# A two-layer decoder step on one core: a new instruction order at the gates and the second head, and the first layer's mixing weights masked and summed in pieces on GpSimd

## The chip, the core and the metric

The kernel runs on one core of a Trainium2 chip. The core has five engines that run side by side, each with its own queue of instructions in order: TensorE (PE; PEld is its weight load), VectorE (DVE), ScalarE (ACT), GpSimd (POOL) and SyncE (SP), which here issues the DMAs. Engines wait for each other through semaphores. The metric is the device time of one execution in microseconds, as the median of several runs; the profile shows one profiled execution, whose span is the time from the first to the last instruction.

## The reference, cut to what matters

One inference step of a two-layer decoder for 256 prompt tokens and 8 x 8 sample tokens (320 columns in all), in float32. The first layer mixes tokens by a causal spatial-gating MLP in chunks of 128:

```python
h = gelu(x @ w_in);  u, v = split(h, 2)
v = layernorm(v) * ln_g + ln_b
ws = where(tril(ones(L, L)), w_s[:, :L, :L], 0)          # 8 groups, L = 128
mixed = einsum('gts,bnsgd->bntgd', ws, v) + b_s
y = (u * mixed) @ w_out
```

The second layer is an mLSTM with 8 heads. Its gates give, per token, the running sum `b` of log-sigmoids and the running maximum `m`; the heads use them as weights:

```python
D = b[:, None] - b[None, :] + i[None, :];  m = max(b + m_prev, max(D))
sc = (q @ k.T) * exp(D - m);  num = exp(b + m_prev - m) * (q @ C) + sc @ v
C_new = decay * C + (k * g).T @ v
```

`q` and `k` go through a causal width-4 convolution and silu, the head's output through a normalisation and a sigmoid gate `o`. Each layer is followed by a gated MLP with a width-3 convolution.

## The kernel before

**Tiling.** The activations stand transposed, features on partitions and the 320 tokens in columns. Every weight matrix is cut into blocks of 128 output rows by 8 x 128 inputs. Products are made to float32 accuracy from two rounded parts: ScalarE casts a loaded block `raw` to the high part `wh` (line 178), VectorE subtracts to get the low part `wl` (line 179), and TensorE adds three products per 128 inputs, high x high, high x low, low x high, so a block of 8 is 24 matmuls of 320 columns. `take` gives the next block in a fixed list and at that point traces the split of the block after it. In the second layer (`low_last`) a block does its 16 matmuls with `wh` first and its 8 with `wl` last. Three pairs of `wh` and `wl` are kept.

**Order.** The kernel is written with a scheduler that orders each engine's instructions by readiness and by the order in which they are traced. TensorE's instructions are pinned to the traced order. Three aids bend the rest: `behind(x, y)` puts x after y in their engine's queue; `with issue_after(y)` does this for everything traced in the block on y's engine; neither makes an engine wait for another. PSUM has eight banks: five tiles of tag `pa`, three of tag `pm`; the blocks of weights use `pm`.

**First layer.** The value half is made first (`group`, tile `pv_a`), then its statistics (`v_stats`: line 452 gives the reciprocal deviation `rstd` on GpSimd), `normalise` on ScalarE (line 458), and 16 blocks of the other half (tile `pm`), between which `mix` multiplies the normalised values with the masked mixing weights `ws` (128 x 8 groups x 128) and, for the samples, `wss`. `load_ws` loads these, masks them on GpSimd (lines 384 and 386), and sums `ws` over partitions into `rsum` (line 387), which `mix` uses with the layer norm's shift. In the profiled execution GpSimd does line 384, then 387, then 386.

**Gates and first head.** `gates` (lines 711 to 814) takes seven blocks in this order: q(0), v(0,0), k(0), v(0,1), o(0,0), o(0,1), and q(1) of the second head; the numbers are head and half. Among them VectorE works out the gate rows: two scans over tokens (line 766 the sum, line 771 the maximum, into `M`), `m` (772), `wi` (778, 779) and `g` (787, 788). ScalarE takes exponentials of them (780, 789, 790, 791) into `Xf` and `RS`. `Xf` is split into two rounded parts in `X` (783, 784), which one matmul broadcasts to all partitions (`pMb`); `RS` is turned by three transposes (`pt`) after q(1). The convolution of k(0) on VectorE is three times line 832 (the last is `S[0]["conv"]`), its product with the tanh is `q_` (836, 838), its split gives `kh` and `khl`; `low` in `gates` is that last subtraction. `last_low` is at any time the newest traced `wl`, `raised` is line 789.

**Later heads.** The loop at the end of `layer_b` does, for head h, the blocks of head h and the rest of head h-1 between them. For h = 1: k(1), v(1,0), `inter` and `numer` of head 0 (tile `num`), `state_prompt` (`pCp`), the first of four pairs of `state_sample` (`pcs`; VectorE's update of C, line 1067, frees the two banks, one of them of tag `pm`), v(1,1), o(1,0), the second pair, `scores(1)` (`psc`), o(1,1), the third pair, `finish(0)` (`phn`), the fourth pair, then the key transposes `k_nat` (`pk`, in a bank of tag `pm`) and `v_nat` (`pv`). `scores` ends with the split of the weighted scores into `Ph` and `Pl`; `o_epi` (line 1075) reads an output-gate block and so frees its bank; `v_epi` (855, 856) does so for a value block.

## Time and profile before

| what | value |
| --- | --- |
| median of 3 runs | 878.53 us (877.89 to 879.15) |
| profiled execution's own time | 878.1 us |
| its span | 876.4 us |
| granted TensorE clock | 0.999 |
| matmuls | 6388 |
| VectorE, ScalarE, GpSimd busy | 675.9, 505.8, 139.4 us |
| DMA | 155.74 MB, mean 178 GB/s |

A row of the timeline reads: start and duration in us, engine, line, operation, out<-in, shapes, how many instructions it merges, and in brackets the idle time of the engine before it and what ended it. The duration of an instruction overlaps that of its neighbours by some 0.07 to 0.16 us, so distances are taken from start to start. A row of the windows has the stretch, its length, and the busy time of PE, PEld, DVE, ACT and POOL with instruction counts, then TensorE's clock, the DMA share and GB/s.

### The profile page before, as it was taken

Reading aid. Unit: us, or ns where it says so; the run is one execution under the profiler, and the core shown is the slowest. Engines: PE = TensorE matmul, PEld = TensorE weight load, DVE = VectorE, ACT = ScalarE, POOL = GpSimd, SP = SyncE. Lnnn points to the kernel's source line nnn. Section 1 sums busy time; section 2 is a strip of 40 time slices with the busy share of each in tenths; the row PEclk is TensorE's granted clock in tenths of the full one; section 3 lists DMA queues with packets and bytes.
Section 4 is the critical chain, followed back from the end, with each engine's and each line's share of the span. In section 5 each row is a group of like instructions: output and inputs, shape, how many; then the busy total and the mean of one; then the engine's idle time right before and its main releaser. Section 6 shows DMA issues by size and latency. Waiting matters only on the chain.

```text
span 876.4 us, 16929 instructions
## 1 busy us (share of the span) xinstructions
PE 869.8 (99%) x6388; PEld 852.4 (97%) x6388; DVE 675.9 (77%) x1304; ACT 505.8 (58%) x917; POOL 139.4 (16%) x289
## 2 busy tenths in 40 slices
PE   9999999999999999999999999999999999999997
PEld 7899999999999999999999999999999999999997
DVE  6866986588878864559999997878998888786443
ACT  7557554455555544446868775656766555554442
POOL 3240000031000000015443222303003000000000
PEclk9999999999999999999999999999999999999999
DMA  8755645545545555554746876565664554455551
GB/s 270 228 193 166 184 146 180 175 148 170 163 155 167 164 163 156 167 177 149 239 147 217 255 226 221 188 211 172 196 218 148 170 168 150 163 163 166 157 151 60
DMA packets 54949, 155.74 MB, mean 178 GB/s; under 512 B 7460, under 2 KB 12716, under 8 KB 54868
## 3 DMA queue, kind: packets, MB, share of 16 engines
q1 hardware_dynamic: 54868, 154.67, 55.9%
q8 instruction: 50, 0.82, 0.4%
q14 instruction: 31, 0.25, 0.1%
HBM read 142.66 MB, written 11.99 MB: 176 GB/s over the span
## 4 chain that ended last, share of the span: by engine, by line
PE 97%; DMA 1%; DVE 1%; ACT 1%; issue 0%; POOL 0%; ACTq 0%
PE pm L81 84%; PE pv_a L81 6%; PE num L81 2%; PE pmix L81 1%; PE pcs L81 1%; PE pCp L81 1%; PE pv L84 1%; PE psc L81 1%; PE phn L84 1%; DMA out_Cp<-Cp 0%; DMA xT<-in_xv 0%; PE pk L84 0%; DVE y_p L665 0%; ACT hn L1039 0%; DVE wl L179 0%
## 5 line engine op out<-in xcount | busy, mean ns | idle before, releaser
L179 DVE TENSOR_TENSOR wl<-raw,wh 128x1024 fp32r<-128x1024 f32 (+4 forms) x254 | 302.7, 1194 | 109.0 <-ACT wh L178 106.2
L178 ACT CAST wh<-raw 128x1024 fp32r<-128x1024 f32 (+4 forms) x254 | 255.5, 1006 | 210.2 <-PE pm L81 146.9
L81 PE MATMUL pm<-xh,wh 128*128 128x320 f32 x1216 | 356.3, 301 | 0.0
L81 PE MATMUL pm<-xl,wh 128*128 128x320 f32 x1216 | 354.5, 299 | 0.0
L81 PE MATMUL pm<-xh,wl 128*128 128x320 f32 x1216 | 308.9, 299 | 0.0
L81 PEld LDWEIGHTS pm<-xh,wh 128*128 128x128 f32 x1216 | 229.9, 189 | 0.6 <-issue 0.5
L81 PEld LDWEIGHTS pm<-xl,wh 128*128 128x128 f32 x1216 | 229.9, 189 | 0.0
L81 PEld LDWEIGHTS pm<-xh,wl 128*128 128x128 f32 x1216 | 211.9, 189 | 0.1
L81 PE MATMUL pm<-yh_f,wh 128*128 128x320 f32 x352 | 105.2, 299 | 0.0
L81 PE MATMUL pm<-yl_f,wh 128*128 128x320 f32 x352 | 105.2, 299 | 0.0
L81 PE MATMUL pm<-yh_f,wl 128*128 128x320 f32 x352 | 105.2, 299 | 0.0
L81 PEld LDWEIGHTS pm<-yh_f,wh 128*128 128x128 f32 x352 | 66.5, 189 | 0.0
L81 PEld LDWEIGHTS pm<-yl_f,wh 128*128 128x128 f32 x352 | 66.5, 189 | 0.0
L81 PEld LDWEIGHTS pm<-yh_f,wl 128*128 128x128 f32 x352 | 66.5, 189 | 0.0
L569 DVE SCALAR_TENSOR_TENSOR fcv<-fpad,vecs,fcv 128x336 f32<-128x336 f32 x88 | 49.2, 565 | 1.4
L571 ACT ACTIVATE fgl<-fcv 128x256 f32<-128x256 f32 x44 | 18.2, 415 | 37.3 <-DVE fcv L569 37.3
L81 PE MATMUL pm<-yh_a,wh 128*128 128x320 f32 x128 | 38.4, 300 | 0.0
L81 PE MATMUL pm<-yl_a,wh 128*128 128x320 f32 x128 | 38.3, 299 | 0.0
L81 PE MATMUL pm<-yh_a,wl 128*128 128x320 f32 x128 | 38.3, 299 | 0.0
L323 DVE TENSOR_TENSOR xT<-pm,xT 128x320 f32<-128x320 f32 x39 | 19.1, 490 | 24.2 <-PE pm L81 24.2
L81 PE MATMUL pm<-yhb,wh 128*128 128x320 f32 x128 | 35.9, 304 | 0.0
L81 PE MATMUL pm<-ylb,wh 128*128 128x320 f32 x128 | 35.5, 300 | 0.0
(268 smaller groups left out, 1266.6 us busy)
## 6 DMA issues: line engine op xcount, KB each, us to landing
raw<-in_f_up SPq DMA_DIRECT2D x88, 512.0 KB, 3.5
raw<-in_b_win SPq DMA_DIRECT2D x48, 512.0 KB, 4.3
raw<-in_f_dn SPq DMA_DIRECT2D x32, 448.0 KB, 3.3
C<-in_C SPq DMA_DIRECT2D x32, 258.0 KB, 5.1
out_Cs<-C SPq DMA_DIRECT2D x32, 258.0 KB, 4.2
raw<-in_a_win SPq DMA_DIRECT2D x16, 512.0 KB, 3.8
raw<-in_a_wo SPq DMA_DIRECT2D x16, 512.0 KB, 4.0
raw<-in_f_dn SPq DMA_DIRECT2D x16, 512.0 KB, 3.5
```

What stands on the lines that cost most here:

```text
L81: self.pin(self.nc.tensor.matmul(out, lhsT, rhs, start=start, stop=stop, skip_group_check=skip))
L84: self.pin(self.nc.tensor.transpose(out, in_, ident))
L178: self.last_split = self.hold(nc.scalar.copy(wh[:, :kn, :], raw[:, :kn, :]))
L179: self.last_low = nc.vector.tensor_tensor(wl[:, :kn, :], raw[:, :kn, :], wh[:, :kn, :].bitcast(F32), op=SUB)
L323: self.nc.vector.tensor_tensor(x, ps[:, :T], x, op=ADD)
L569: nc.vector.scalar_tensor_tensor(cv, pd[:, i:i + NC], self.vec(w + i * KF), cv, op0=MULT, op1=ADD)
L571: nc.scalar.activation(gl[:, :TP], cv[:, :TP], AF.Gelu_apprx_tanh)
```

## The change

It has three parts. In the first layer the mask of `ws` is made in four instructions of two groups each, the sum over partitions too, and the sums are queued behind the last mask of `wss`. In the gates the copy of `Xf` to `X` (line 783) and the copy within `RS` (line 794) go from VectorE to GpSimd; the scan of line 771 is queued behind the newest `wl` at that point (that of o(0,1)), which was so for the last convolution step of k(0); line 784 is queued behind `low`; the edge to `again` goes. In the second head the scores come ahead of the second pair of `state_sample`, and `Pl` of the second head is queued behind the `o_epi` of o(1,1).

```diff
                 with tc.issue_after(self.rc_made.ins):
-                    nc.gpsimd.tensor_tensor(ws, ws, trit.unsqueeze(1).to_broadcast([P, NH, P]), op=MULT)
+                    pairs = [slice(g, g + 2) for g in range(0, NH, 2)]
+                    for g in pairs:
+                        nc.gpsimd.tensor_tensor(ws[:, g], ws[:, g], trit.unsqueeze(1).to_broadcast([P, 2, P]), op=MULT)
                     for r, c in quads:
-                        nc.gpsimd.tensor_tensor(wss[r, :, c], wss[r, :, c], bdt[r].unsqueeze(1).to_broadcast([64, NH, 64]), op=MULT)
-                    nc.gpsimd.partition_all_reduce(rsum.rearrange("p g t -> p (g t)"), ws.rearrange("p g t -> p (g t)"), P, ReduceOp.add)
+                        made = nc.gpsimd.tensor_tensor(wss[r, :, c], wss[r, :, c], bdt[r].unsqueeze(1).to_broadcast([64, NH, 64]), op=MULT)
+                    with tc.issue_after(made.ins):
+                        for g in pairs:
+                            nc.gpsimd.partition_all_reduce(rsum[:, g].rearrange("p g t -> p (g t)"), ws[:, g].rearrange("p g t -> p (g t)"), P, ReduceOp.add)
...
-                nc.vector.tensor_tensor_scan(M, rst[:8, 1, :], aM, -1e30, op0=ADD, op1=MAX)
+                scan = nc.vector.tensor_tensor_scan(M, rst[:8, 1, :], aM, -1e30, op0=ADD, op1=MAX)
...
-                nc.vector.tensor_copy(X[0:8], Xf)
-                nc.vector.tensor_tensor(X[32:40], Xf, X[0:8].bitcast(F32), op=SUB)
+                nc.gpsimd.tensor_copy(X[0:8], Xf)
+                Xl = nc.vector.tensor_tensor(X[32:40], Xf, X[0:8].bitcast(F32), op=SUB)
...
-                again = nc.vector.tensor_copy(RS[:64, T:384], RS[:64, TP:T])
+                again = nc.gpsimd.tensor_copy(RS[:64, T:384], RS[:64, TP:T])
...
-                self.behind(S[0]["conv"], self.last_low)
-                with tc.issue_after(S[0]["conv"].ins), tc.issue_after(raised.ins), tc.issue_after(again.ins):
+                self.behind(scan, self.last_low)
+                with tc.issue_after(S[0]["conv"].ins), tc.issue_after(raised.ins):
                     ps = self.block(KD, self.x_rhs)
                 for q_ in S[0]["q_"]:
                     self.behind(q_, self.last_low)
+                self.behind(Xl, low)
...
                 self.split(Ph[:, :384], Pl, Pf[:, :384])
+                s["Pl"] = self.parts[1]
...
             def o_epi(h, j, ps):
-                nc.vector.tensor_tensor(o, ps[:, :T], self.rb, op=MULT)
+                made = nc.vector.tensor_tensor(o, ps[:, :T], self.rb, op=MULT)
...
+                return made
...
                 if h == 1:
                     o_epi(h, 0, blk())
+                if h == 1:
+                    scores(h)
                 if h:
                     made = state_sample(h - 1, order[1])
...
-                scores(h)
+                if h != 1:
+                    scores(h)
...
                 if h and not last:
-                    o_epi(h, 1, blk())
+                    o_made = o_epi(h, 1, blk())
                 if h == 1:
+                    self.behind(S[1]["Pl"], o_made)
                     state_sample(0, order[2])
```

## The prediction

> **What bounds the kernel now.** I read the page first: its span and busy times.
>
> ```profile
> span 876.4 us, 16929 instructions
> PE 869.8 (99%) x6388; PEld 852.4 (97%) x6388; DVE 675.9 (77%) x1304; ACT 505.8 (58%) x917; POOL 139.4 (16%) x289
> ```
>
> TensorE is busy for 869.8 of 876.4 us. The change removes no matmul, so it can gain only what TensorE loses between matmuls in the stages touched, and lose only where it makes TensorE wait anew. A busy share hides small losses (matmuls overlap in the records), so I went through TensorE's timeline and compared the distance of neighbouring starts with the distance usual for that shape. The usual distances come from the chain of work in order of time (start, duration, what):
>
> ```profile
> 4.48 56.05 PE pv_a L81 x272
> 60.53 16.30 PE pm L81 x120
> ...
> 413.74 0.33 PE pt L84 x3
> ...
> 456.41 0.73 PE psc L81 x7
> ...
> 464.59 0.22 PE pcs L81 x2
> ```
>
> A 320-column matmul takes 16.30 / 120 = 0.136 us, one of the state update 0.22 / 2 = 0.11. In the first layer the value phase and the five blocks behind it join without a gap (4.48 + 56.05 = 60.53). So **the first layer has no TensorE loss that its part of the change could win back.** In the gates and in the second head the timeline shows three places:
>
> ```profile
> 408.92 0.30 PE L81 MATMUL pm<-xl,wh 128*128 128x320 f32 x1
> 409.13 1.35 PE L81 MATMUL pm<-xh,wl 128*128 128x320 f32 x8
> 410.32 0.30 PE L81 MATMUL pm<-xh,wh 128*128 128x320 f32 x1
> ...
> 432.22 0.27 PE L81 MATMUL pcs<-vh,kgz 128*128 128x258 f32 x1
> 432.90 0.38 PE L81 MATMUL pcs<-vh,kgz 128*128 128x258 f32 x1 [0.41 <-DVE C L1067]
> ...
> 437.95 0.47 PE L81 MATMUL pcs<-vb,kgz 128*128 128x258 f32 x2
> 438.53 0.55 PE L84 MATMUL pk<-ident,qs 128*128 128x128 f32 x3
> ...
> 464.34 0.47 PE L81 MATMUL pcs<-vb,kgz 128*128 128x258 f32 x2
> 464.65 0.49 PE L84 MATMUL pk<-ident,qs 128*128 128x128 f32 x3
> ```
>
> - **A**, in o(0,1), where the low parts of the weights begin: 408.92 to 409.13 is 0.21 where 0.14 is usual, and the first of the eight (1.35 us together, 0.27 + 8 x 0.135) takes about 0.10 more. Loss 0.17 us.
> - **B**, first head's state update: 432.22 to 432.90 is 0.68 instead of 0.11, and the second matmul is 0.38 instead of 0.27. Loss 0.57 + 0.10 = 0.67 us. It waits for VectorE's update of C, which frees the PSUM bank.
> - **C**, ahead of the second head's key transposes: 437.95 to 438.53 is 0.58; the third head does the same step in 0.31 (464.34 to 464.65); with 0.55 instead of 0.49 behind it, the loss is 0.33 us.
>
> A + B + C = **1.17 us, 0.13% of the time**: that is all that can be won. About 0.2%, 1.76 us, is what a measurement of this kernel can tell from no change.
>
> **The change part by part: the gates.** On VectorE and on ScalarE the stretch looks so:
>
> ```profile
> 406.37 0.54 DVE L832 SCALAR_TENSOR_TENSOR bcv<-bpad,vecs,bcv 128x344 f32<-128x344 f32 x1
> 406.84 0.48 DVE L772 TENSOR_TENSOR g<-g,Xf 8x320 f32<-8x320 f32 x1
> ...
> 407.87 1.20 DVE L179 TENSOR_TENSOR wl<-raw,wh 128x1024 fp32r<-128x1024 f32 x1
> 409.00 0.56 DVE L832 SCALAR_TENSOR_TENSOR bcv<-bpad,vecs,bcv 128x344 f32<-128x344 f32 x1
> 409.49 0.34 DVE L783 CAST X<-Xf 8x392 fp32r<-8x392 f32 x1
> ```
>
> ```profile
> 401.30 1.04 ACT L178 CAST wh<-raw 128x1024 fp32r<-128x1024 f32 x1
> ...
> 407.36 0.41 ACT L790 ACTIVATE RS<-g 8x256 f32<-8x256 f32 x1 [2.68 <-DVE g L772]
> ...
> 408.36 0.47 ACT L789 ACTIVATE RS<-g 8x320 f32<-8x320 f32 x1
> 408.85 1.05 ACT L178 CAST wh<-raw 128x1024 fp32r<-128x1024 f32 x1
> ```
>
> Loss A is the subtraction wl at 407.87: it ends at 409.07, and the low sweep of o(0,1) wants it at 408.92 + 0.14 = 409.06. Its own cast is old (401.30), so it could have run earlier. The change puts the scan (L771) behind this wl instead of the convolution's last step. The wl then runs two microseconds sooner and A goes: **-0.17 us**.
>
> The same edge delays the scan, m (L772), the rows behind it, and the exponentials on ScalarE, which wait for m (2.68 us idle at 407.36). Behind the last of them, `raised` (408.36), stands the cast wh at 408.85, which ends at 409.90 and is that of q(1); the edge that holds it there is kept. TensorE starts q(1) at 410.32, and 0.17 earlier without A: 410.15. So the cast has 0.25 us to spare. The delay of the scan is unknown; ends: if the wl takes the place of the convolution step at 406.37, 1.13 (its distance to the next start, 409.00 - 407.87) less 0.47 (406.84 - 406.37) = 0.66 us; if the third step, now free, slips in too, 1.13 + 0.49 = 1.62 us. The wait at q(1) is the delay less 0.25: **0.41 to 1.37 us**. I take the wl alone, the one row the new edge forces: 1.13 - 0.25 = **+0.88 us**.
>
> The copy of X (L783, 0.34 us) and a smaller one go to GpSimd, and Xl goes behind the key's low part. That frees VectorE after the exponentials, where the path runs through ScalarE's cast; I count nothing. Both ends of the copies are covered: their first reader is the transpose pt at 413.74, 3.9 us after X is copied now (409.83), and the broadcast of X comes later still; beyond that they would cost what they are late.
>
> **The second head.** VectorE's and ScalarE's rows:
>
> ```profile
> 432.37 0.47 DVE L1067 SCALAR_TENSOR_TENSOR C<-C,dec,pcs 128x258 f32<-128x258 f32 x1
> ...
> 437.39 0.56 DVE L334 TENSOR_TENSOR Pl<-Pf,Ph 128x384 fp32r<-128x384 f32 x1 [0.21 <-ACT Ph L334]
> ...
> 438.00 0.48 DVE L1075 TENSOR_TENSOR o_b<-pm,rb 128x320 f32<-128x320 f32 x1
> ```
>
> ```profile
> 433.09 0.21 ACT L856 COPY vTb<-pm 128x64 f32<-128x64 f32 x1
> ```
>
> With the scores ahead of the update, TensorE has 0.73 us of work (psc, seven matmuls) from 432.22, and the bank is free at 432.37 + 0.47 = 432.84, before the update comes at 432.95: B goes, -0.67. What is late next is the bank of o(1,1): TensorE now gets there at 432.95 + 0.22 = 433.17, and v(1,1) leaves its bank at 433.30. I add 0.10, between 0 and 0.20 (an eviction's end to the next start). Loss C is the wait for o_b (438.00 to 438.48), which frees the bank; it sat behind Pl. With Pl behind o_b, o_b can start at about 437.3 when its block is through, ends before 437.95, and C goes: -0.33. Pl is late by 0.45 us; its first reader, the next `numer`, stands behind two blocks of 24 x 0.136 = 3.26 us each. Together **-0.90 us**.
>
> **The first layer.** Here the question is only whether the new order makes something late.
>
> ```profile
> 34.69 3.36 POOL L384 TENSOR_TENSOR ws_a<-ws_a,trit 128x1024 f32<-128x1024 f32 x1 [3.54 <-DMA trit<-in_trit]
> 43.64 7.43 POOL L387 PARTITION_ALL_REDUCE rs_a<-ws_a  x1 [5.59 <-issue]
> 58.85 2.61 POOL L386 TENSOR_TENSOR wss_a<-wss_a,bdt 64x512 f32<-64x512 f32 x2 [7.78 <-issue]
> 67.55 0.91 POOL L452 TENSOR_TENSOR rstd_a<-ve_a,mhalf 128x3 f32<-128x3 f32 x1 [6.08 <-DVE ve_a L451]
> ```
>
> ```profile
> 34.59 4.54 DVE L179 TENSOR_TENSOR wl<-raw,wh 128x1024 fp32r<-128x1024 f32 x2 [0.23 <-ACT wh L178]
> ...
> 47.19 3.37 DVE L179 TENSOR_TENSOR wl<-raw,wh 128x1024 fp32r<-128x1024 f32 x1 [2.11 <-ACT wh L178]
> ...
> 72.02 1.22 DVE L179 TENSOR_TENSOR wl<-raw,wh 128x1024 fp32r<-128x1024 f32 x1 [2.45 <-ACT wh L178]
> ```
>
> A wl takes 1.2 us, but 3.37 beside the sum over partitions, and two take 4.54 beside the mask: GpSimd holds VectorE up, and pieces shorten the hold. TensorE loses nothing from it now, so that is worth 0. [...]
>
> What can be late is rstd (67.55). Two idle stretches without a releaser, 5.59 and 7.78 us, stand before and after the sum. Before, the second one ended 8.7 us ahead of rstd; in the new order it comes last. Masks 34.69 to about 42 (3.36 + 2.61 = 5.97 of work, and waits for one or two wl), then 5.6, the four sums R, then 7.8: GpSimd is ready at 55.4 + R. R lies between 7.43 (cost goes by size) and 4 x 7.43 = 29.7 (cost goes by call). I take the lower end with 2 us of waits for wl, R = 9.4, since the masks' cost goes by size; GpSimd is ready at 64.8, before 67.55: **0 us**.
>
> **Sum**: -0.17 + 0.88 - 0.90 = **-0.19 us**. Against the profiled execution's own 878.1 us (876.4 of span and 1.7 around it) that is 877.9; that execution lies 0.4 below the median of the runs, 878.5, so I forecast a median of **878.3 us**. With the ends of the unknown terms (0.41 to 1.37, 0 to 0.20) the sum goes from -0.76 to +0.40: 877.8 to 878.9.
>
> **The rivals.**
> - **R1, the gates cost nothing.** The scan's new place is paid from a step that moves behind it, and q(1)'s cast keeps its time. Against it: 0.25 us to spare and 0.66 at least. For it: the scan's neighbours (L832) are free to move. All three losses go: -1.07 to -1.17, 877.4 us.
> - **R2, the second head's waits come back elsewhere.** VectorE is nearly full there:
>
> ```profile
> 414.00:440.00 26.00, 25.48 (x205) 24.30 (x204) 25.04 (x64) 21.86 (x56) 11.70 (x25) 1.00 0.76 242
> ```
>
>   It is busy for 25.04 of 26.00 us, so another eviction may become late. Then the gates' 0.88 to 1.37 less 0.17 stays: +0.7 to +1.2, 879.2 to 879.7 us. Against it: the two waits have named releasers, and each is moved out of the way.
> - **R3, rstd becomes late (slower).** Its place is the first layer, 67 to 74 us:
>
> ```profile
> 68.68 1.52 ACT L458 ACTIVATE v_a<-v_a,ve_a,rstd_a 128x512 f32<-128x512 f32 x2 [2.06 <-DVE ve_a L453]
> ...
> 70.96 1.03 ACT L178 CAST wh<-raw 128x1024 fp32r<-128x1024 f32 x1
> ```
>
> ```profile
> 73.68 0.30 PE L81 MATMUL pm<-xh,wl 128*128 128x320 f32 x1
> ```
>
>   The normalisation waits for rstd, the cast at 70.96 stands behind it, the wl at 72.02 behind that, done at 73.24, and TensorE wants it at 73.68. So rstd has 0.4 us to spare; beyond 67.95 TensorE loses every microsecond. That is from R = 12.5, or 1.7 us of fixed cost for each sum after the first; at 3 us for each, R = 16.4 and the time is 4 us longer, 882 us. No row shows a second sum; against it speaks that the masks have hardly any fixed cost. If every sum brought its own 5.6 us, three more would make it 14 to 17 us, 892 to 895 us (1 in 100; the loads are pairs of instructions around a change of kind, and the sums follow each other). [...]
>
> **How the numbers follow.** Forecast 0.45, R1 0.26, R2 0.17, R3 0.12 (a quarter of it under 1.5 us). The range 877.0 to 880.0 takes in the forecast's ends, R1 and R2 with the 0.6 us by which runs of before differ from their median, and leaves out most of R3. Faster by over 0.2% (under 876.8) would need more than the three losses hold: 0.03, from R1. Slower by over 0.2% (over 880.3) is R3's larger part and a little of R2: 0.11. Within: 0.86.
>
> **What would show it.** Gates: the wl of o(0,1) ends before 408 and its low sweep starts without a gap; `raised` ends after 409.2, and TensorE waits for a cast ahead of q(1). If there is no such wait, R1 holds. Second head: seven score matmuls at the place of the 0.68 us step, and pk 0.3 us behind pcs. First layer: wl no longer over about 2.5 us; one idle stretch before the first sum, none between sums; rstd at 67.5. A rstd after 68 and a gap on TensorE near 73.7 would prove R3 and me wrong.

## The result and the profile after

The changed kernel takes **882.26 us** (median of 6 runs, 880.68 to 882.91) against 878.46 us for the kernel before (6 runs on the same chip, 877.89 to 879.15): a ratio of 1.0038, interval [1.0027, 1.005]. The change makes the kernel 3.8 us slower; 878.3 us had been forecast, and 880.0 us was the end of the range.

The page of the profiled execution (882.1 us by itself) begins with its span, and gives the busy time of each engine:

```profile
span 880.4 us, 16936 instructions
...
PE 870.2 (99%) x6388; PEld 852.4 (97%) x6388; DVE 673.8 (77%) x1302; ACT 506.6 (58%) x917; POOL 137.2 (16%) x297
```

The span is 4.0 us longer and TensorE is busy only 0.4 us longer, so the time went into new TensorE waits. The view of what the engines wait for lists them (waiting engine and line, releaser, total us, times, longest):

```profile
PE pm L81 <- ACT wh L178: 1.4, 1, 1.4
PE phn L84 <- ACT hn L1045: 1.3, 1, 1.3
PE pv_a L81 <- ACT v_a L417: 1.1, 1, 1.1
```

None of the three is in the profile before. The line numbers of the changed kernel are a little higher than those of before (the scan L775, `m` L776, the convolution L837, C's update L1073, `nb` L1038, `hn` L1045, `o_b` L1081). By the first layer's wait, everything in the second layer is also 1.34 us later than before: the convolution step at 405.15 is now at 406.49. Differences below are taken after that shift.

**At q(1).** TensorE's timeline around the wait, then VectorE's and ScalarE's:

```profile
410.39 1.25 PE L81 MATMUL pm<-xh,wl 128*128 128x320 f32 x8
413.02 0.40 PE L81 MATMUL pm<-xh,wh 128*128 128x320 f32 x1 [1.38 <-ACT wh L178]
```

```profile
406.49 0.56 DVE L837 SCALAR_TENSOR_TENSOR bcv<-bpad,vecs,bcv 128x344 f32<-128x344 f32 x1
406.98 1.21 DVE L179 TENSOR_TENSOR wl<-raw,wh 128x1024 fp32r<-128x1024 f32 x1
...
408.60 0.81 DVE L775 TENSOR_TENSOR_SCAN Xf<-rst,g 8x320 f32<-8x320 f32 x1
409.34 0.54 DVE L837 SCALAR_TENSOR_TENSOR bcv<-bpad,vecs,bcv 128x344 f32<-128x344 f32 x1
409.81 0.47 DVE L776 TENSOR_TENSOR g<-g,Xf 8x320 f32<-8x320 f32 x1
```

```profile
409.92 0.49 ACT L839 ACTIVATE bth<-bcv 128x344 f32<-128x344 f32 x1 [3.90 <-DVE bcv L837]
...
411.93 1.04 ACT L178 CAST wh<-raw 128x1024 fp32r<-128x1024 f32 x1
```

The eighth matmul of the first row starts at 411.34 and q(1) should start 0.14 behind it; it starts at 413.02, 1.54 us late, and its first matmul is 0.10 longer: **1.65 us**. VectorE shows why. The `wl` of 406.98 is ahead of the scan, and the convolution's third step (409.34), now free, has slipped in ahead of `m` as well. So `m` is 409.81 - 406.84 - 1.34 = 1.63 us later. On ScalarE the tanh `bth`, which stood behind the cast before, now runs ahead of the exponentials, and the cast `wh` starts 411.93 - 408.85 - 1.34 = 1.74 us later.

**In the second head.** TensorE's timeline, then VectorE's and ScalarE's:

```profile
435.37 0.56 PE L81 MATMUL psc<-qs 128*128 128x128 f32 x4
435.73 0.47 PE L81 MATMUL pcs<-vh,kgz 128*128 128x258 f32 x2
...
439.30 0.39 PE L81 MATMUL pcs<-vh,kgz 128*128 128x258 f32 x2
441.01 1.57 PE L84 MATMUL phn<-ident,hn 128*128 128x128 f32 x6 [1.32 <-ACT hn L1045]
442.34 0.47 PE L81 MATMUL pcs<-vb,kgz 128*128 128x258 f32 x2
442.64 0.49 PE L84 MATMUL pk<-ident,qs 128*128 128x128 f32 x3
```

```profile
436.57 0.48 DVE L1081 TENSOR_TENSOR o_b<-pm,rb 128x320 f32<-128x320 f32 x1
436.97 1.21 DVE L179 TENSOR_TENSOR wl<-raw,wh 128x1024 fp32r<-128x1024 f32 x1
438.10 0.55 DVE L905 SCALAR_TENSOR_TENSOR Pf<-psc,w 128x384 f32<-128x384 f32 x1
...
438.70 0.86 DVE L1073 SCALAR_TENSOR_TENSOR C<-C,dec,pcs 128x258 f32<-128x258 f32 x2
...
439.62 0.15 DVE L1038 SCALAR_TENSOR_TENSOR nb<-mv,sl 128x3 f32<-128x3 f32 x1
```

```profile
439.25 0.80 ACT L885 ACTIVATE w<-Mb,cols 128x256 f32<-128x256 f32 x2
...
440.39 1.48 ACT L1045 ACTIVATE hn<-num,nb,sl 128x256 f32<-128x256 f32 x3
```

In the profile before, the same steps on TensorE and VectorE were:

```profile
437.38 0.82 PE L84 MATMUL phn<-ident,hn 128*128 128x128 f32 x6
```

```profile
434.11 0.48 DVE L1075 TENSOR_TENSOR o_b<-pm,rb 128x320 f32<-128x320 f32 x1
434.51 0.87 DVE L1067 SCALAR_TENSOR_TENSOR C<-C,dec,pcs 128x258 f32<-128x258 f32 x2
435.29 0.15 DVE L1032 SCALAR_TENSOR_TENSOR nb<-mv,sl 128x3 f32<-128x3 f32 x1
```

B is gone: the two `pcs` matmuls now take 0.47 us together, behind the scores. C is gone: `pk` starts 0.30 behind the last `pcs`. In their place stands a larger wait. The second `pcs` of 439.30 starts at 439.41; the transposes `phn` should follow 0.11 later and start at 441.01, 1.49 us late; and the six take 1.57 instead of 0.82 us, because the three pieces of `hn` come one by one: **2.24 us**. Their input `hn` needs `nb`, and `nb` is queued behind the second pair's update of C. That update has moved with its matmuls behind the scores, and in VectorE's queue behind a `wl` and the scores' `Pf`. ScalarE adds to it: `nb` ends at 439.77, but `w` and a cast of `Ps` stand ahead of `hn`, which starts at 440.39.

**In the first layer**, GpSimd's sums and `rstd`:

```profile
46.79 7.42 POOL L391 PARTITION_ALL_REDUCE rs_a<-ws_a  x4 [6.05 <-issue]
68.51 0.90 POOL L456 TENSOR_TENSOR rstd_a<-ve_a,mhalf 128x3 f32<-128x3 f32 x1 [14.31 <-DVE ve_a L455]
```

GpSimd is done with the four sums at 54.21 and stands idle until `rstd`, whose releaser is VectorE's `ve_a`. The first layer's own wait comes from elsewhere, as ScalarE's and TensorE's timelines show:

```profile
22.25 1.04 ACT L178 CAST wh<-raw 128x1024 fp32r<-128x1024 f32 x1 [2.02 <-DMA raw<-in_a_wv]
```

```profile
32.72 0.38 PE L81 MATMUL pv_a<-wh,xh 128*128 128x512 f32 x1
34.19 0.48 PE L81 MATMUL pv_a<-wh,xh 128*128 128x512 f32 x1 [1.09 <-ACT v_a L417]
```

A block of weights came late: its cast stood 2.02 us for the DMA, and starts at 22.25 instead of 20.77, before the first instruction that the change touches. The squares behind it on ScalarE, `rc`, which is made from them, and `v_a`, which waits for `rc`, are late with it. TensorE lost about 1.36 us (34.19 - 32.72 - 0.21, and 0.10 of the next matmul).

| TensorE's loss (us), profiled executions | before | after |
| --- | --- | --- |
| A, low sweep of o(0,1) | 0.17 | 0 |
| q(1) | 0 | 1.65 |
| B, state update | 0.67 | 0 |
| `phn` | 0 | 2.24 |
| C, key transposes | 0.33 | 0 |
| first layer, late weights | 0 | 1.36 |
| sum | 1.17 | 5.25 |

The difference, 4.08 us, is that of the spans, 4.0.

### The profile page after: what moved, and what is told of

The parts are those of the page before. It is cut to its first block, busy times and chain, and to the rows that moved or that the text cites. A ratio compares the mean times of both kernels' runs of the same rounds, so it can differ in the third digit from the quotient of the medians.

```text
span 880.4 us, 16936 instructions
## 1 busy us (share of the span) xinstructions
PE 870.2 (99%) x6388; PEld 852.4 (97%) x6388; DVE 673.8 (77%) x1302; ACT 506.6 (58%) x917; POOL 137.2 (16%) x297
## 4 chain that ended last, share of the span: by engine, by line
PE 92%; DVE 3%; DMA 2%; ACT 1%; issue 1%; POOL 1%; SPq 0%; ACTq 0%; DVEq 0%
PE pm L81 82%; PE pv_a L81 3%; PE num L81 2%; DMA raw<-in_a_wv 2%; PE pmix L81 1%; DVE wl L179 1%; PE pcs L81 1%; PE pCp L81 1%; PE phn L84 1%; PE pv L84 1%; PE psc L81 1%; POOL nr L297 1%; ACT wh L178 0%; DVE bcv L837 0%; PE pk L84 0%
```

## The experiments

All times are medians, with those of the kernel before from the same chip beside them. The diffs are against the kernel before unless it is said otherwise, and `e2`, `e3` and so on stand for the full names.

### The three parts, each alone

`e1_first_layer_only`: the part in `load_ws`, nothing else.

```diff
-                    nc.gpsimd.tensor_tensor(ws, ws, trit.unsqueeze(1).to_broadcast([P, NH, P]), op=MULT)
+                    for g in pairs:
+                        nc.gpsimd.tensor_tensor(ws[:, g], ws[:, g], trit.unsqueeze(1).to_broadcast([P, 2, P]), op=MULT)
...
+                    with tc.issue_after(made.ins):
+                        for g in pairs:
+                            nc.gpsimd.partition_all_reduce(rsum[:, g].rearrange("p g t -> p (g t)"), ws[:, g].rearrange("p g t -> p (g t)"), P, ReduceOp.add)
```

> Only the first layer's part of the change. Theory: the 1.3 us that TensorE waits near 32.7 us in the profile of the changed kernel comes from a weight block that landed late (ScalarE's cast waited 2.02 us for it at 22.25), 10 us before GpSimd's first new instruction, so this part is worth nothing: median within 0.7 us of before, 877.8 to 879.2, rstd_a at about 67.5, no wait of TensorE near 73.7. Rival: the new GpSimd order makes the first layer slower: 879.7 to 880.2, with the wait near 32.7 in most executions.

Measured: 878.51 us against 878.47 (12 and 35 runs), ratio 1.0002 [0.9991, 1.0012]. Its profile has A, B and C as before and no wait near 32.7; `rstd` starts at 67.14. The theory held: the part is worth nothing either way.

`e2_gates_only`: the edits in `gates`, nothing else.

```diff
+                scan = nc.vector.tensor_tensor_scan(M, rst[:8, 1, :], aM, -1e30, op0=ADD, op1=MAX)
...
-                self.behind(S[0]["conv"], self.last_low)
-                with tc.issue_after(S[0]["conv"].ins), tc.issue_after(raised.ins), tc.issue_after(again.ins):
+                self.behind(scan, self.last_low)
+                with tc.issue_after(S[0]["conv"].ins), tc.issue_after(raised.ins):
```

> Only the gates' part. Theory: the scan behind wl, and with it the third convolution step and the tanh ahead of the exponentials, makes the cast of q(1)'s block 1.6 to 1.75 us later, TensorE waits about 1.6 us for it, loss A (0.17) goes, the second head's 1.0 us stays: 879.7 to 880.2. Rival: the second head's waits shrink by what TensorE came late: 878.5 to 879.0.

Measured: 880.25 us against 878.47, ratio 1.0018 [1.0008, 1.0028]. TensorE's timeline has the wait at q(1):

```profile
412.97 0.40 PE L81 MATMUL pm<-xh,wh 128*128 128x320 f32 x1 [1.37 <-ACT wh L178]
```

The theory's mechanism held. A is gone, but B has shrunk to 0.32 us, which it had not foreseen (the two `pcs` take 0.54 us to the next start, 0.22 without a wait).

`e3_head_only`: the edits in the second head, nothing else.

```diff
+                s["Pl"] = self.parts[1]
...
+                if h == 1:
+                    scores(h)
                 if h:
                     made = state_sample(h - 1, order[1])
...
-                scores(h)
+                if h != 1:
+                    scores(h)
...
-                    o_epi(h, 1, blk())
+                    o_made = o_epi(h, 1, blk())
                 if h == 1:
+                    self.behind(S[1]["Pl"], o_made)
```

> Only the second head's part. Theory: the update of C, and the row nb that is queued behind it, come behind a wl and the weighted scores on VectorE, so hn is late and TensorE waits about 2.2 us for it at the transposes phn, while the two old losses (0.67 and 0.33) go: 879.4 to 880.0. Rival: hn is late only because the gates made everything late; here alone the part gains 0.9: 877.3 to 877.9.

Measured: 880.51 us against 878.47, ratio 1.002 [1.0009, 1.003]. `hn` is late in this kernel too, with the gates and the first layer as before. The view of waits lists it, and no wait at q(1):

```profile
PE phn L84 <- ACT hn L1040: 1.4, 1, 1.4
```

The time is 0.5 us over the theory's range; four of the twelve runs belong to an upper group, of which more below.

The three medians add up: 0.04 + 1.78 + 2.04 = 3.86 us, and the whole change costs 3.80. Each part's interval reaches 0.9 us either way, so that the sums agree this closely is luck.

### The gates: the edge, and what stands behind it

`e4_gates_no_scan_edge`: as `e2`, but the convolution's last step and not the scan is queued behind the `wl`, as before.

```diff
-                self.behind(scan, self.last_low)
+                self.behind(S[0]["conv"], self.last_low)
```

> The gates' part without the edge on the scan: the last convolution step is behind wl as before, the two copies on GpSimd, Xl behind khl. Theory: the edge alone makes the wait at q(1), so without it the time is before's or up to 0.3 better, 877.9 to 878.7, loss A of 0.17 us still there. Rival: the copies on GpSimd make X or RS late and cost by themselves: above 879.2, with a wait of TensorE at pt or pMb.

Measured: 878.71 us against 878.47, ratio 1.0 [0.9991, 1.001]; its profile has no wait at q(1). The moves to GpSimd cost nothing that can be measured; the edge on the scan is the cost of the part. The moves also do something that the prediction put at nothing: B is only 0.19 us here. The next start is 433.82, so the two matmuls take 0.41 us instead of 0.22.

```profile
433.41 0.57 PE L81 MATMUL pcs<-vh,kgz 128*128 128x258 f32 x2
```

VectorE's update of C starts 0.33 us before the first of them (at 433.08); in the kernel before, it started 0.15 us after it. The two copies, 0.38 us from start to start (409.49 to 409.87), are off VectorE's queue. That this is what lets the update come earlier is argued from these distances and not tested alone.

`e6_gates_cast_free`: as `e2`, with the scan's edge, but q(1)'s cast is no longer held behind the exponentials.

```diff
-                with tc.issue_after(S[0]["conv"].ins), tc.issue_after(raised.ins):
+                with tc.issue_after(S[0]["conv"].ins):
                     ps = self.block(KD, self.x_rhs)
```

> The gates' part alone, as in e2_gates_only, but the cast of q(1)'s block is no longer queued behind the last of the exponentials on ScalarE. Theory (q(1) waits 1.53 us because its cast stands behind exponentials that the later scan has made late): the wait at 411.3 us goes although the scan stays late; A is gone; time 878.2 to 878.6 us, unless the exponentials' readers (pt, pMb behind q(1)) become late, which I put at 0 to 0.5 us. Rival (the scan's lateness itself costs, through the rows that TensorE needs next, or something else of this part does): TensorE waits over 1 us for RS or X at about 413 to 415 us, time 879.5 us or more.

Measured: 878.05 us against 878.78 (11 and 29 runs), ratio 0.9988 [0.9979, 0.9997]. ScalarE's timeline shows the cast ahead of the first exponential, which starts at 410.53:

```profile
409.60 1.03 ACT L178 CAST wh<-raw 128x1024 fp32r<-128x1024 f32 x1
```

TensorE waits for nothing between 404 and 416 us, although the scan is as late as in `e2`. So the later scan alone costs nothing: its readers `pt` and `pMb` have the time. What cost 1.65 us was a cast that needs none of the exponentials and stood behind them by an edge. A is gone in this profile, and so is all of B but 0.04 us, which had not been expected; most of B went already in `e4`. C stays.

### The second head: where nb stands

`e5_head_nb_early`: as `e3`, but the first head's `nb` and `hn` are queued behind the first pair's update of C.

```diff
                 if h == 1:
+                    with tc.issue_after(made.ins):
+                        normed(h - 1)
                     scores(h)
                 if h:
                     made = state_sample(h - 1, order[1])
-                    if not last:
+                    if not last and h > 1:
```

> The second head's part alone, as in e3_head_only, but the normalisation of the first head (nb, hn) is queued behind the FIRST pair's update of C, ahead of the scores, and no longer behind the second pair's. Theory (the part costs because nb and hn stand behind the update of C that the scores were put ahead of): the wait of phn for hn (2.36 us in e3_head_only) goes, the waits B (0.67 us) and C (0.33 us) of the kernel before go too, A (0.17 us) stays; span about 875.4 us, time 877.4 to 877.9 us (0.6 to 1.1 us under the kernel before). Rival (hn is late because VectorE and ScalarE are nearly full in this stretch whatever the order, so that another eviction takes the place): a new wait of TensorE of over 1 us between 432 and 442 us, time 879.0 us or more.

Measured: 881.05 us against 878.78, ratio 1.0028 [1.0017, 1.0039], slower than `e3`. The wait for `hn` is gone and another one of nearly the same size is there; C is not gone either (`pk` starts 0.87 us behind `pcs`). VectorE, ScalarE and TensorE in the profile (about 5 us later here, by a first-layer wait):

```profile
439.09 0.16 DVE L1033 SCALAR_TENSOR_TENSOR nb<-mv,sl 128x3 f32<-128x3 f32 x1 [0.84 <-POOL sl L1024]
```

```profile
439.29 0.56 ACT L1040 ACTIVATE hn<-num,nb,sl 128x256 f32<-128x256 f32 x1 [1.22 <-DVE nb L1033]
```

```profile
440.33 0.40 PE L81 MATMUL pm<-xh,wh 128*128 128x320 f32 x1 [1.66 <-ACT vTb L856]
```

`nb` was now too early: VectorE waited in it for GpSimd's `sl`, and on ScalarE the first piece of `hn` stood in front of the copies of v(1,1) (`vTb`, from 439.75), which free the bank that o(1,1) needs. The rival held for this order: an eviction became late. Whether any order does better is the next question.

`e9_head_nb_behind_o`: as `e3`, but `nb` directly behind the reading of o(1,0).

```diff
+                    o_first = o_epi(h, 0, blk())
                 if h == 1:
+                    with tc.issue_after(o_first.ins):
+                        normed(h - 1)
                     scores(h)
```

> The second head's part alone, as in e3_head_only, but nb of the first head is queued directly behind the reading of o(1,0) (o_b), instead of behind the second pair's update of C. In e3_head_only GpSimd has its input sl ready at 434.81 us and that o_b ends at 434.48, so VectorE stands for about 0.4 us ahead of a subtraction that nobody wants soon, and hn runs on ScalarE in the idle 1.13 us ahead of Ph, behind the copies of v(1,1). Theory (the 2.36 us wait of phn comes from nb's place in the queue alone; e5_head_nb_early failed only because it put nb ahead of wl and o_b, where it waited 0.84 us for sl and hn then held the copies of v(1,1)): the wait of phn goes, no other comes; B and C gone; span 875.4 to 875.9 us, time 877.3 to 877.9 us. Rival (the stretch has no room: any place of nb makes another eviction late): a new TensorE wait of over 1 us between 432 and 445 us, 879 us or more.

Measured: 879.07 us against 878.87 (12 and 29 runs), ratio 1.0004 [0.9996, 1.0013]: 1.8 us less than `e3` against the kernel before. The wait of `phn` and B are gone, and no wait of over 1 us has come in the second head; so the place of `nb`, and of `hn` behind it, is the cause. But the time is that of the kernel before and not 1 us less. VectorE and TensorE in its profile (about 3.5 us later by a first-layer wait):

```profile
438.49 0.16 DVE L1033 SCALAR_TENSOR_TENSOR nb<-mv,sl 128x3 f32<-128x3 f32 x1 [0.36 <-POOL sl L1024]
```

```profile
441.06 0.54 PE L81 MATMUL pcs<-vb,kgz 128*128 128x258 f32 x2
441.76 0.55 PE L84 MATMUL pk<-ident,qs 128*128 128x128 f32 x3 [0.16 <-DVE o_b L1076]
```

The 0.36 us in which VectorE stands for `sl` make all behind it late, `o_b` too, and `pk` starts 0.70 behind `pcs` again: C is back. Neither theory had that, though the time is the rival's.

### Loss C alone

`e7_pl_edge_only`: the kernel before, with `Pl` behind `o_b` alone.

```diff
+                    self.behind(S[1]["Pl"], o_made)
```

> The kernel before with one edge alone: Pl of the second head is queued behind the reading of o(1,1) (o_b). Theory: C (0.33 us ahead of the key transposes pk) goes and nothing else changes: span 876.0 to 876.1 us, ratio 0.9996. Rival (that wait comes back at a later place because VectorE is nearly full there): C goes and as much appears elsewhere behind it; span 876.3 us or more.

Measured: 879.20 us against 878.78, ratio 1.0009 [0.9999, 1.002]. C is gone at `pk`, and 0.44 us appear one block later (444.61 is 0.48 behind the last of the eight matmuls before it, instead of 0.14, and its first is 0.10 longer). TensorE and VectorE there:

```profile
443.18 1.25 PE L81 MATMUL pm<-xh,wl 128*128 128x320 f32 x8
444.61 0.40 PE L81 MATMUL pm<-xh,wh 128*128 128x320 f32 x1 [0.18 <-DVE C L1068]
```

```profile
443.12 1.04 DVE L1097 SCALAR_TENSOR_TENSOR ylb<-y_b,gnh,yhb 128x320 fp32r<-128x320 f32 x2 [0.95 <-ACT yhb L1096]
444.08 0.48 DVE L1068 SCALAR_TENSOR_TENSOR C<-C,dec,pcs 128x258 f32<-128x258 f32 x1
```

The fourth pair's second update of C frees the next block's bank. It stood behind `ylb`, and VectorE waited 0.95 us for ScalarE ahead of `ylb`. In the kernel before, loss C covered this.

A further 0.30 us is lost ahead of the block that follows `pv`: it starts 0.87 us after the first transpose of `pv` (440.03), in the kernel before 0.57. TensorE and VectorE:

```profile
440.90 0.40 PE L81 MATMUL pm<-xh,wh 128*128 128x320 f32 x1
```

```profile
439.52 0.54 DVE L334 TENSOR_TENSOR Pl<-Pf,Ph 128x384 fp32r<-128x384 f32 x1
439.99 0.86 DVE L1068 SCALAR_TENSOR_TENSOR C<-C,dec,pcs 128x258 f32<-128x258 f32 x2
```

`Pl` now stands ahead of the third pair's update of C, and the block starts right where that update ends (440.85). So the edge on `Pl` wins 0.33 and loses 0.30 + 0.44 us; the 0.41 us that this makes is close to the 0.42 of the medians, though the interval is wider than that. That the third pair's update is what this block waits for is read from the two times. The rival held.

### Versions put together

`e8_all_mended`: gates as in the change, but with the convolution's second step behind the `wl` in place of the scan; head as in `e5`.

```diff
+                self.behind(S[0]["conv2"], self.last_low)
...
+                    with tc.issue_after(made.ins):
+                        normed(h - 1)
                     scores(h)
```

> Both parts mended, the first layer as in the kernel before. Gates: the two copies on GpSimd and the split of X behind the key's low part stay, but it is the convolution's SECOND step, not the scan, that is queued behind the wl of o(0,1). Second head: scores early and Pl behind o_b as in the changed kernel, but the first head's normalisation is queued behind the first pair's update of C. Theory (each part loses only by what stands behind the instruction that was moved): A, B and C go and no wait takes their place; 1.17 us less than before, span 875.2 us, time 877.2 to 877.6 us, which is faster than both kernels. Rival (gates and second head are so full on VectorE that any order gives the losses back): 878.4 us or more.

Measured: 881.85 us against 878.78, ratio 1.0038 [1.0023, 1.0053]. At the second head it has the fault of `e5`. At q(1) TensorE waits again, and loses 1.29 us with the longer first matmul. A `wl` ahead of `m` is 1.13 us whatever edge puts it there, and the cast has 0.25 to spare; the tanh `bth`, which the convolution's earlier end lets in among the exponentials (409.08, 0.49 us), makes the cast later by some 0.4 more. Both mends were wrong, and by its time the rival held.

`e10_gates_and_head`: the gates of `e6` and the head of `e9`.

> The gates as in e6_gates_cast_free (the changed kernel's gates without the edge that holds q(1)'s cast behind the exponentials) and the second head as in e9_head_nb_behind_o; first layer as before. Theory: the two parts do not touch, A, B and C are all gone and no wait is left: span 875.2 to 875.5 us, time 877.0 to 877.5 us, faster than both kernels. Rival (the gates' part had already removed B by shifting the head's work, so that the head's part adds only its costs): as e6_gates_cast_free or slower, 877.9 us or more.

Measured: 878.15 us against 878.87, ratio 0.9995 [0.9986, 1.0004]; 0.72 us less, the same as `e6` alone, as the rival had it. A and B are gone and C nearly so, but 0.28 and 0.10 us stand where `e7` has its wait at `ylb`, and 0.30 us ahead of the block behind `pv`, as in `e7`.

`e12_last_pair_first`: as `e10`, and `ylb` behind the fourth pair's update of C (diff against `e10`).

```diff
                     finish(h - 1)
-                    state_sample(h - 1, 3)
+                    made = state_sample(h - 1, 3)
+                if h == 1:
+                    for y in S[0]["ylb"]:
+                        self.behind(y, made)
```

> As e10_gates_and_head, and in the second head the two subtractions ylb are queued behind the fourth pair's update of C. In e10_gates_and_head and e7_pl_edge_only TensorE waits about 0.45 us (0.28 and 0.10 at 441.93 in the former) for a bank that this pair's second update frees; the update stood behind ylb, which itself waited 0.88 us for ScalarE's yhb. Theory (C was won at pk and lost again there): that wait goes, span 875.4 to 875.6 us, time 0.9 to 1.2 us under the kernel before, that is 877.6 to 877.9 us if the kernel before is at 878.8. Rival (the next step is bound by something else, the casts on ScalarE or the bank of another tile): TensorE loses as much within the next 3 us and the time is that of e10_gates_and_head, 0.7 us under the kernel before.

Measured: 877.83 us against 878.81 (12 and 29 runs), ratio 0.9988 [0.9976, 1.0], 0.98 us less. VectorE does both of this pair's updates in one stretch from 439.65, ahead of `ylb` (440.99), and the wait that the other update had caused is gone: the theory held. Of C about 0.1 us is left at `pk`, and the 0.30 us ahead of the block behind `pv` (438.86) stay, since the third pair's update is still behind `Pl`. This version is faster than both kernels by its median, though the interval reaches to no change.

`e11_after_cast_free`: the changed kernel with the one edge of `e6` less. `e13_after_both_mended`: that, and `nb` as in `e9`.

> The changed kernel whole, with one edge less: q(1)'s cast is not held behind the exponentials. Theory: its 1.65 us wait at q(1) goes and everything else stays, the 2.2 us at phn too: 1.5 to 1.7 us less than the changed kernel's 882.3, that is 880.5 to 880.8 us. Rival (with the cast early, the exponentials and what reads them become late in the whole change): 881.5 us or more.

> The changed kernel whole with both queue places mended: q(1)'s cast not held behind the exponentials (as in e11_after_cast_free) and nb directly behind the o_b of o(1,0) (as in e9_head_nb_behind_o). The first layer in pieces stays. Theory (the two queue places are all that the change costs): as e10_gates_and_head, 0.6 to 0.8 us under the kernel before. Rival (the first layer's part costs something that shows only in the whole change): 0.8 us or more over that, slower than the kernel before.

Measured: `e11` 879.08 us against 878.87, ratio 1.0005 [0.9996, 1.0015]; `e13` 877.82 us against 878.81, ratio 0.9987 [0.9977, 0.9998]. With both places in the queues mended, the whole change, first layer included, is about 1 us faster than the kernel before. `e11` came out 1.4 us below its theory's lower end, on which the next runs bear.

### The rest: the granted clock

`e14_changed_again`: the changed kernel.

> The changed kernel, unchanged, again. Its six runs fell into two groups, 880.7 (two runs) and 882.1 to 882.9 (four), and its profiled run, of the second group, holds a wait of 1.26 us in the first layer, at 32.72, for a block of weights that came late. Theory (that wait comes by chance, as in the profiles of kernels whose first layer is the old one): most of the twelve runs here lie near 2.8 us over the kernel before, few near 4. Rival (the first layer's new order brings it): half of them or more lie 3.6 to 4.5 us over the kernel before.

Measured: 882.37 us against 878.81. The twelve runs fall into two groups: five from 880.71 to 881.34 and seven from 882.36 to 882.72. By the counts, the theory that the upper group is made by weights that come late by chance falls. But the first layer is not the cause either, since `e11` and `e13`, which have the same first layer, do not show it: eleven of the twelve runs of `e11` lie between 878.80 and 879.42. The mean granted clock of the runs does differ: 0.998 to 1.000 in the lower group and 0.996 to 0.998 in the upper. `e3`, with the old first layer, has the like: four of its twelve runs, from 881.43 to 882.12 us, have a clock of 0.997, the other eight, up to 880.82, one of 0.998 to 1.000.

What a lower clock may follow from, the first layer of `e11`'s profile shows. There TensorE stands idle for 2.35 us (6.00 - 3.65) in the first of these two stretches (stretch, length, busy time of PE, PEld, DVE, ACT, POOL, granted clock, DMA share, GB/s):

```profile
30.00:36.00 6.00, 3.65 (x18) 2.87 (x17) 4.05 (x8) 0.89 (x2) 5.92 (x6) 1.00 0.90 281
36.00:41.00 5.00, 5.00 (x16) 4.08 (x17) 4.93 (x8) 4.27 (x7) 1.67 (x2) 0.66 0.10 30
```

Behind the wait the clock is 0.66 for 5 us. So the question was whether the wait at `phn` does the same.

`e15_nb_later`: the changed kernel with `nb` one step later, so that this wait is longer (diff against the changed kernel).

```diff
-                    if not last:
+                    if not last and h > 1:
                         with tc.issue_after(made.ins):
                             normed(h - 1)
...
-                    state_sample(0, order[2])
+                    made = state_sample(0, order[2])
+                    with tc.issue_after(made.ins):
+                        normed(0)
```

> The changed kernel with nb of the first head queued one step later still, behind the third pair's update of C: hn starts about 1.3 us later, so TensorE's wait for the first hn grows from about 1.5 to about 2.8 us (about 3.5 us with the gaps between the three pieces). In the changed kernel's twelve runs of e14_changed_again the five near 881.0 us have a mean granted clock of 0.998 to 1.000, the seven near 882.4 one of 0.996 to 0.998, and in the first layer of e5_head_nb_early a wait of 2.85 us is followed by a stretch of 5 us in which the granted clock is 0.66. Theory (a wait as long as that at phn makes the clock gate halve TensorE's clock for about 3.4 us in some executions, 1.5 us, and in more the longer the wait): nearly all runs at a clock of 0.996 to 0.998, time about 881.0 + 1.3 + 1.5 = 883.8 us, and the profile shows a granted clock under 1 behind phn. Rival (the upper group has another cause): two groups as before, about 882.3 and 883.7 us, with the lower one as frequent.

Measured: 884.01 us against 878.78 (7 and 11 runs), ratio 1.0053 [1.0032, 1.0073]. Six of the seven runs have a mean granted clock of 0.993 to 0.997, the seventh 0.998, and no lower group is left. In the profile (an execution of 889.12 us, which has the first layer's wait too) TensorE's timeline and the window behind `phn` are:

```profile
445.56 2.02 PE L84 MATMUL phn<-ident,hn 128*128 128x128 f32 x6 [2.88 <-ACT hn L1045]
```

```profile
446.00:450.00 4.00, 4.00 (x19) 3.72 (x19) 2.40 (x7) 2.30 (x6) 0.19 (x1) 0.50 0.56 166
```

The clock is 0.50 behind the wait, and the six transposes take 2.02 us instead of the changed kernel's 1.57. The theory held for this longer wait, and its time, 883.8, too. The theory's half clock over 3.4 us, an estimate, comes to the 1.7 us of full clock that 5 us at 0.66 lose (5 x 0.34, first layer of `e5`), and its 1.5 us to the distance of the two groups (881.0 and 882.4). Here the clock was lower for longer: it is 0.85 over 442 to 446, 0.50 over 446 to 450 and 0.79 over 450 to 454, and the matmuls of 320 columns from 449.99 to 450.79 stand 0.27 us apart, where 0.136 is usual.

`e16_changed_look`: the changed kernel once more, for one profile.

> The changed kernel, one more profiled execution. If it falls near 882.4 us, the theory of the clock expects a granted clock under 1 in the few us behind the wait of phn (439 to 446 us) and nothing in the first layer; the rival expects a wait in the first layer as in the first profile (1.26 us at 32.72). If it falls near 881 us it tells nothing of this.

Measured: 880.75 us, clock 0.999, of the lower group; it tells nothing of the upper one. No profile of the changed kernel itself shows this lower clock, so that its upper group has this cause is inferred from its lower mean clock, from `e15`, and from `e11`, where the wait at `phn` is a little shorter (1.1 instead of 1.3 us) and the group is gone.

Two things speak against the wait's length alone: `e3` waits as long at `phn` (1.4 us) and has only four of twelve runs in its upper group, and in `e5` two runs with a clock of 0.996 (880.93 and 881.05 us) take no longer than the others. So this part stays open.

## Why the prediction was wrong, step by step

- **What can be won (A + B + C = 1.17 us): right.** All three went in the changed kernel. `e12`, where some 0.4 us of them comes back, is 0.98 us faster by its median.
- **Gates, A (-0.17 us): right.** The `wl` ends at 408.19 - 1.34 = 406.85, ahead of the 408 named.
- **Gates, the scan's delay (+0.88 us): the mechanism right, the size wrong.** `e4` shows that the edge is the cost, and `e6` that it acts through the cast behind `raised`. The prediction had the ends 0.41 and 1.37 and took "the wl alone, the one row the new edge forces". But the third convolution step did slip in (`m` is 1.63 us later, the upper end's 1.62), and `bth` moved ahead of the exponentials; the wait was 1.65 us. With the `wl` alone ahead of `m`, as in `e8`, it was 1.29 us and not 0.88: the term left out what moves on ScalarE. R1, in which q(1) does not wait, fell.
- **The copies on GpSimd (0): right for the time** (`e4`), but "I count nothing" missed that B shrinks with them, to 0.19 us in `e4`. The two parts share that gain.
- **Second head, B (-0.67) and C (-0.33): right in the changed kernel. "What is late next is the bank of o(1,1)" (+0.10): this is the step that failed.** That bank cost nothing in the changed kernel and 0.14 us in `e3`. Late next was `hn`, 2.24 us. The prediction followed the moved matmuls on TensorE and the banks that they share, and did not follow what is queued behind their eviction. The second pair's update of C moves with its matmuls, and `nb` is held behind that update by an edge in the code. Before, `nb` started at 435.29; in the changed kernel at 439.62, 4.33 us later. The reading of o(1,0) in the same queue is 2.46 us later (434.11, 436.57), from the late weights and q(1); the other 1.87 us come from the new order. `e3` alone has the same wait. The term was not -0.90 but -1.00 + 2.24 = +1.24 us.
- **R2** named the right kind of event, an eviction that becomes late on a full VectorE, at a chance of 0.17. But its price was only that the won microsecond would not come; `nb` was no part of it. And it was the queue's order that made `nb` late and not the load: in `e9` the same work in another order has no wait at `phn`.
- **C alone** was counted as won. `e7` shows that the edge on `Pl` costs 0.30 + 0.44 us just behind it. In the changed kernel these do not show, since TensorE comes late there from `phn`: that C came out as forecast is luck.
- **First layer (0): right**, by `e1`. The four sums took 7.42 us together, the lower end of R (7.43), and 8.35, 8.39 and 8.61 in `e1`, `e13` and `e11`, under the 9.4 taken; `rstd` waited for VectorE and not for GpSimd; R3 fell. `rstd` came at 68.51, after the 68 that was to prove R3, but 1.34 us of that is the late weights, and TensorE has no gap at its place. The `wl` beside the sums took 2.25 and 1.66 us (48.53 and 52.93), under the 2.5 named. No run shows the 2 us of waits for `wl` that the 9.4 holds: these four profiles leave at most 1.2 us (8.61 - 7.43) over the one sum. R3's pairs of instructions are two `MODIFY_POOL_CONFIG` at 38.0 ahead of the sum and two at 51.0 ahead of line 386, in the views of lines 387 and 386 of before; in the changed kernel 6.05 us of idle time stand ahead of the first of the four sums, and none between them.
- **The median.** -1.17 + 1.65 + 2.24 = +2.72 us fits the profiles without late weights: the spans of `e14` and `e16` are 879.2 and 879.0 us, 2.8 and 2.6 over the 876.4 of before. The five lower runs of `e14` lie 1.9 to 2.5 us over the median of before on their chip. The median of the six runs is drawn up to 3.8 by upper runs: three have a clock of 0.996 or 0.997, and the profiled one, at 0.999, has the late weights instead. That the lower clock follows from the wait at `phn` is inferred. No step of the prediction had such a thing: it priced waits at their length alone.

## What to carry to other kernels

When a group of instructions is moved, go through every edge that hangs on its last instruction, on every engine: here a three-column `nb`, held behind the update of C, cost more than the three waits that were removed. A wait that is removed may have covered another one just behind it (0.44 us in `e7`), so look one block further for the next bank to come free. And a wait of TensorE can cost more than its length: behind waits of 2.35 and 2.88 us its clock was 0.66 over 5 us (`e11`) and 0.50 over 4 us (`e15`) here.

## What the runs showed of the hardware that was not expected

- The granted TensorE clock fell after a wait within the kernel: to 0.66 over 5 us after 2.35 us without work (`e11`), to 0.50 over 4 us after 2.88 us (`e15`). It did not always do so. In the first layer of `e9`, with a wait of 2.9 us, TensorE was busy for 0.52 of 3 us and the clock stayed at 1.00 (columns as above):

```profile
33.00:36.00 3.00, 0.52 (x3) 0.12 (x1) 2.89 (x6) 0.36 (x1) 2.23 (x1) 1.00 0.90 248
36.00:39.00 3.00, 2.62 (x12) 2.31 (x13) 2.74 (x5) 3.00 (x5) 0.00 (x0) 1.00 0.28 112
```

- Four sums over partitions of 256 columns took 7.42 us together, one of 1024 took 7.43 in the kernel before; in `e1`, `e13` and `e11` the four took 8.35, 8.39 and 8.61 us. Idle time of about 6 us stood ahead of the first alone (6.05; 6.30 in `e1`, 6.17 in `e13`).
- In at least five of the profiled executions TensorE waits between 30 and 40 us for `v_a`, by the view of waits: 2.7 and 2.9 us in kernels with the old first layer (`e5`, `e9`), 1.1, 2.3 and 2.6 us in those with the new one (after, `e11`, `e15`). In four of these, ScalarE's cast of a block near 22 us stood for its weights, 1.46 us in `e5`, 2.02, 1.28 and 1.58 in the three others; in `e9` it stood 1.71 us for TensorE. What decides it stayed open.
